# All eleven sums of down-projection weights made in the out-projection, in raw weight buffers

## The chip, the cores and the metric

The kernel runs on one core of a Trainium2 chip. The metric is the device time of one execution in microseconds (us); the time before is 2308.32 us, the median of 3 runs (2305.21 to 2309.71). All five engines of the core are in use: TensorE (PE, with its weight loads PEld), VectorE (DVE), ScalarE (ACT), GpSimd (POOL) and SyncE (SP), whose queue issues nearly all DMAs.

## The reference, cut to what matters

The kernel computes one layer of a streaming encoder for 2048 prompt tokens and 8 x 16 sample tokens, all in float32:

```python
x @ w_in -> heads (mLSTM with chunkwise state, sliding-window attention)
mix = concat(heads) @ w_out
h = layer_norm(ALPHA * x + mix)
u = h @ w_up                       # value | gate, 2 x 2816 wide
c = causal depthwise convolution of u, width 3
f = (silu(gate) * value) @ w_down  # 2816 x 1024
y = layer_norm(ALPHA * h + f)
```

Only one thing in it is touched by the change: sums of blocks of `w_down`. The big products are done by a seven-product scheme in the manner of Strassen, which needs sums and differences of quarters of the weights. For the down-projection these are made ahead of time, once, and kept in DRAM.

## The kernel before, in words

**Stages.** The program is Python that writes out every instruction. Four stages follow each other: the input projection (`i_dense`, four blocks of 512 tokens, the first with the sample tokens, 5 groups of weights), the out-projection (`o_block`, five blocks `OBLOCKS` of 3, 4, 4, 4 and 2 tiles of 128 tokens), the up-projection with the convolution (`f_ups`), and the down-projection (`f_downs`). The attention and mLSTM work of the heads runs as three chains (`t_sample`, `m_chain`, `a_chain`) that `Chains.weave` puts between the steps of the dense stages, by costs and latencies written into their `yield`s.

**Float32 in three products.** Each operand is split by `split` (L216) into a rounded part (a copy on ScalarE, L218) and a rest (a subtraction on VectorE, L219); three matmuls stand for one.

**What sets the order.** TensorE's order is that of the program text (`manual_schedule`). The instructions of the other engines, SP's DMA issues among them, are ordered by a scheduler at compile time: among what is ready, what comes earlier in the program goes first, and a DMA may go far ahead of its place if its buffer is free. On the chip each engine then works strictly through its own list. A tile of a pool has a tag, and as many buffers as the tag has; a new tile waits until an earlier one with that tag has had its last use.

**Out-projection** (L1588, `o_block`, and L901, `group`). A block is done in two halves of the 1024 output columns. A half takes the four units of 512 KB of its weights, which stay in place while the tiles of the block pass by: 8 steps of 3 matmuls (512 columns) a tile, so 24 steps in a half of block 0 and 32 in blocks 1 to 3; `steps` counts them. In the last round of a half (L919) the units are given back, and the next half's are split (`advance`, L415, `next_split`, L465, `next_raw`, L424). In a second half `x_pair` (L885) also brings in and splits the next block's tokens. A result is taken out of PSUM at L1613 and normalised by `norm` (L1562) in pieces, one every second step.

**Raw weights.** They land in `wraw`, a tag of 7 buffers of 512 KB (`WR`), by `raw_slot` (L405) and the DMA at L462, and are split from there. `raw_free` (L410) lets the program text go at most four loads ahead of the splits.

**The sums** (L841, `d_sums(k, step)`). There are 11 (`NK2`). Step 0 loads two 128 x 1024 tiles of `w_down` (L845, L846), step 1 does four subtractions of 128 x 512 on VectorE (L851 to L854), step 2 stores both tiles to `zt` (L856, L857). Before, the tiles `txy` have the tags `xr1` and `xr3`, buffers that the tokens of the input projection and `x_pair` use as well. Eight sums are made in the last two blocks of the input projection, in the four first groups of weights of each (L683); `self.sums` counts them. The other three are made in the first halves of the out-projection's blocks 1, 2 and 3, at steps 2, 14 and 20 (L1607). The down-projection reads `zt` as weights (L2015), from about 1838 us on.

Of the kernel before, what the change touches and what calls it, by code (L numbers as in the profile page):

```python
# [8 lines left out]
F32 = mybir.dt.float32  # L9
# [5 lines left out]
P = 128  # L15
D = 1024
# [21 lines left out]
WR = 7  # L38
# [16 lines left out]
NK2 = NFF // 2  # L55
# [150 lines left out]
class Prog:  # L206
# [381 lines left out]
    def i_dense(self):  # L588
        nc, a = self.nc, self.a
        nb = len(IBLOCKS)  # L590
        last = NG - 1

        self.next_raw()
        self.x_load(0, 2)
        for _ in range(3):
            self.next_raw()
        self.x_load(0, 4)
        self.single_raw = self.tp.tile([P, KD, P], F32, name="xsr", tag="pth", bufs=2)
        nc.sync.dma_start(self.single_raw, a["xs"])
        self.angles = {}  # L600
        self.rope_load(IBLOCKS[0][2], 2)
        self.rope_load(NPT, 1)
        self.next_split()
        self.x_steps(0, "b12")
        for _ in range(3):
            self.next_split()
        self.x_steps(0, 3)
        self.x_single(1, 2)
        self.x_load(0, 1)
        self.next_raw()  # L610
        self.x_load(0, 3)
        self.x_steps(0, 1)
        self.advance()
        self.x_steps(0, 2, "t3", 7, "t2", 6)
        self.x_single(4)
        self.x_steps(0, "t1", 5, "t4")
        self.sb, self.trans = {}, None

        passages = [{1: ["load"], 7: ["t3", 7], 6: ["t2", 6], 3: [3, "t4"], 4: ["b12", "t1"]},
                    {1: ["load"], 6: ["t3"], 7: [7, "t2"], 5: [6], 3: [3, "t4"], 4: ["b12", "t1"]}]  # L620
        sums = 0
        after = None
        for item in self.items:
            if after:

                after[0] -= 1
                if after[0] == 3:
                    self.logs_of(after[1] - 1)
                if after[0] < 0:
                    self.i_done = after[1]  # L630
                    after = None
            self.chains.hold = item[0] == "t" and item[1] > 0
            if item[0] == "t":
                _, b, ti, e = item
                if ("g", e, 3) not in self.wu:
                    self.advance()
                if b not in self.gates:
                    self.gates[b] = self.tp.tile([P, 5, 8], F32, name="gates", tag="gates", bufs=2)
                ps = self.bank([P, 512], "pg") if ti == 4 else self.ib[ti % 2 * 2]
                yield from self.i_direct(b, ti, e, ps)  # L640
                self.i_keys(b, ti, ps)
                if ti == 1:
                    if b + 1 < nb:
                        self.x_steps(b + 1, 1, 2)
                    else:
                        self.release(4)
                    after = [6, b + 1]
                elif ti == 3 and b or ti == 4:
                    self.release(4)
                    self.x_steps(b, 4)  # L650
                    if b:
                        self.x_steps(b, 5)
                self.advance()
                continue
            _, b, g, s = item
            if item not in self.wu:
                self.advance()
            yield from self.i_product(b, g, s)
            del self.wu[item]
            self.release(2)  # L660
            if self.trans and s != 4:
                self.i_transposes()
            with self.tc.high_priority():
                behind = self.i_after(b, g, s)
            if (b, g, s) == (0, 0, 7):
                self.t_setup()
            if (g, s) == (1, 6):
                self.rope_load(IBLOCKS[b][0], 2)
            if g == last and b + 1 < nb:
                if s == 7:  # L670
                    self.rope_load(IBLOCKS[b + 1][2], 2)
                for x in passages[b > 0].get(s, ()):
                    if x == "load":
                        self.spare = True
                        self.x_load(b + 1, 1, 2, 3, 4)
                    else:
                        self.x_steps(b + 1, x)
            if g == last and b + 1 == nb and s in (7, 5, 2, 3):
                self.x_pair(0, (7, 5, 2, 3).index(s))
            with self.tc.issue_after(behind) if behind and b == 0 else nullcontext():  # L680
                self.advance()

            if b >= nb // 2 and g < last:  # L683

                steps = (6, 2, 5) if g == last - 1 else (6, 5, 3)
                if s in steps:
                    self.d_sums(sums, steps.index(s))
                    sums += s == steps[2]
        self.sums = sums
        self.logs_of(nb - 1)  # L690
        self.chains.hold = False

# [148 lines left out]
    def d_sums(self, k, step):  # L841
        nc, V = self.nc, self.nc.vector
        if step == 0:
            self.txy = x, y = [self.xp.tile([P, D], F32, name="txy", tag=f"xr{q}", bufs=1) for q in (1, 3)]
            nc.sync.dma_start(x, self.a["wdn"][k])  # L845
            nc.sync.dma_start(y, self.a["wdn"][NK2 + k])  # L846
            return
        x, y = self.txy
        if step == 1:
            l, r = slice(0, 512), slice(512, D)  # L850
            V.tensor_sub(x[:, l], x[:, r], x[:, l])  # L851
            V.tensor_sub(x[:, r], y[:, r], x[:, r])
            V.tensor_sub(y[:, r], y[:, r], x[:, l])
            V.tensor_sub(y[:, l], y[:, l], y[:, r])  # L854
            return
        nc.sync.dma_start(self.zt[0, k], x)  # L856
        nc.sync.dma_start(self.zt[1, k], y)  # L857
# [730 lines left out]
    def o_block(self, b):  # L1588
        nc, nb = self.nc, len(OBLOCKS)
        tiles = OBLOCKS[b]  # L1590

        ys = self.ynext + [self.o_x(t) for t in tiles[len(self.ynext):]]
        self.ynext = []

        outs = [self.fp.tile([P, D], F32, name="ymix", tag="hst", bufs=2) for _ in tiles] if b == nb - 1 else ys
        for hf in range(2):
            c = slice(hf * 512, hf * 512 + 512)
            steps = 0
            for cost, ti, ps in self.group(b, tiles, 8 * b + 4 * hf, hf == 1):
                yield cost  # L1600
                if ps is None:
                    steps += 1
                    if hf and b + 1 < nb and steps == 8 * len(tiles) - 6:
                        self.ynext = [self.o_x(t) for t in OBLOCKS[b + 1][:2]]
                    if steps % 2 == 0 and self.norms and next(self.norms[0], self) is self:
                        del self.norms[0]
                    if hf == 0 and b and self.sums < NK2 and steps in (2, 14, 20):  # L1607
                        self.d_sums(self.sums, (2, 14, 20).index(steps))
                        self.sums += steps == 20
                    continue  # L1610
                y = outs[ti]
                with self.tc.high_priority():
                    nc.vector.scalar_tensor_tensor(y[:, c], ys[ti][:, c], ALPHA, ps, op0=ALU.mult, op1=ALU.add)  # L1613
                if hf and b == nb - 2 and ti >= len(tiles) - 2:

                    nc.sync.dma_start(self.zh[tiles[ti]], y)
                elif hf and b < nb - 1:
                    self.norms.append(self.norm(y, *self.ln1, self.zh[tiles[ti]]))
        assert b < nb - 1 or self.sums == NK2
        self.late = list(zip(outs, tiles))  # L1620
# [575 lines left out]
```

## Time and profile before

| | us |
|---|---|
| median of 3 runs (lowest, highest) | 2308.32 (2305.21, 2309.71) |
| profiled execution | 2306.25 |
| its span, first to last instruction | 2304.5 |
| busy: PE, DVE, ACT, POOL | 2278.9, 1807.4, 1272.4, 279.4 |
| sums in the input projection, first load to last store's issue | 299.4 to 546.2 (8 sums) |
| sums in the out-projection, likewise | 642.6 to 835.2 (3 sums) |

The profile is of one execution. Times in it are counted from the first instruction. A row of a timeline has the start, the duration, the engine, the line of the kernel, the operation, and the tiles written and read; in square brackets stands how long the engine idled before it and what released it. "w<-wraw" reads: writes `w`, reads `wraw`. A row of the list of waits has the waiting engine and line, what it waited for, the total in us, how often, and the longest. A busy TensorE is a matmul in the pipe; its idle time is what remains of a window.

### The profile page before, as it was taken

To read this page: it belongs to the slowest core of one execution; us is meant where nothing else is said; L and a number is where in the kernel's file an instruction comes from. 1 tells how busy PE (TensorE), PEld (TensorE's weight loads), DVE (VectorE), ACT (ScalarE), POOL (GpSimd) and SP (SyncE) were. 2 spreads that over 40 slices of the span, in tenths; PEclk is the share of its full clock that TensorE was granted. 3 is DMA by queue.
4 is the path that set the end of the run, shared out by engine and by line. 5 is a ranking of instruction groups with operands and counts; after the bars stand their busy time and mean duration, and the time that the engine had idled before them with its cause. 6 is when DMAs were issued, how large, how long until landed. Compare 5 with 4: busy or idle time off the path is not lost.

```text
span 2304.5 us, 39741 instructions
## 1 busy us (share of the span) xinstructions
PE 2278.9 (99%) x14293; PEld 2094.4 (91%) x14293; DVE 1807.4 (78%) x3075; ACT 1272.4 (55%) x2377; POOL 279.4 (12%) x509
## 2 busy tenths in 40 slices
PE   8999999999999999999999999999999999999998
PEld 8999999989877778999999999999999978888876
DVE  8787587787688888998778777678766786895987
ACT  5453476776766656555656555556555544444442
POOL 0001001100011210211112101003111200200200
PEclk9999999999999999999999999999999999999999
DMA  7988999899987757888777888878998786746742
GB/s 267 319 306 297 309 322 342 310 306 341 309 286 239 242 199 277 302 328 300 277 281 272 307 304 310 306 256 289 316 299 260 248 299 213 253 170 223 253 156 83
DMA packets 300165, 632.38 MB, mean 274 GB/s; under 512 B 47868, under 2 KB 141120, under 8 KB 299968
## 3 DMA queue, kind: packets, MB, share of 16 engines
q1 hardware_dynamic: 295296, 616.14, 77.3%
q0 software_dynamic: 3520, 10.56, 1.4%
q10 hardware_dynamic: 1152, 3.15, 0.4%
q8 instruction: 113, 1.85, 0.3%
q14 instruction: 84, 0.69, 0.1%
HBM read 458.11 MB, written 171.64 MB: 273 GB/s over the span
## 4 chain that ended last, share of the span: by engine, by line
PE 81%; DVE 4%; DMA 2%; issue 1%; ACT 1%; POOL 0%; SPq 0%; DVEq 0%; ACTq 0%; POOLq 0%
PE dps L1874 19%; PE fup L1874 19%; PE dps L705 8%; PE fup L2081 6%; PE dps L2081 6%; PE fht L2081 6%; PE dps L223 3%; PE dps L224 2%; PE dps L225 2%; PE ppo L1349 1%; PE psc L1304 1%; PE ppt L1343 1%; PE dps L731 1%; PE fht L1698 1%; PE pscore L1129 1%
## 5 line engine op out<-in xcount | busy, mean ns | idle before, releaser
L1874 PE MATMUL fup<-hh,uw 128*128 128x384 f32 (+1 forms) x1848 | 478.4, 328 | 0.0
L1874 PE MATMUL dps<-hh,uw 128*128 128x384 f32 (+1 forms) x1848 | 478.0, 328 | 0.0
L1874 PEld LDWEIGHTS fup<-hh,uw 128*128 128x128 f32 x1848 | 330.5, 188 | 0.0
L1874 PEld LDWEIGHTS dps<-hh,uw 128*128 128x128 f32 x1848 | 330.3, 188 | 0.0
L1932 DVE SCALAR_TENSOR_TENSOR cc<-u,cw,cc 128x768 f32<-128x768 f32 (+1 forms) x264 | 258.2, 979 | 62.8 <-ACT cc L1930 56.1
L1874 PE MATMUL fup<-hl,uw 128*128 128x384 f32 (+1 forms) x924 | 303.2, 328 | 0.9 <-DVE hl L219 0.9
L1874 PE MATMUL dps<-hl,uw 128*128 128x384 f32 (+1 forms) x924 | 302.8, 328 | 0.0
L705 PE MATMUL dps<-w,oh 128*128 128x256 f32 x1344 | 254.2, 284 | 0.0
L218 ACT CAST uw<-wraw 128x1024 fp32r<-128x1024 f32 x126 | 123.3, 979 | 230.4 <-PE dps L2081 122.4
L219 DVE TENSOR_TENSOR w<-wraw,w 128x1024 fp32r<-128x1024 f32 (+2 forms) x167 | 189.7, 1142 | 66.0 <-ACT w L218 61.9
L218 ACT CAST w<-wraw 128x1024 fp32r<-128x1024 f32 (+2 forms) x167 | 163.0, 984 | 119.0 <-PE dps L705 61.9
L705 PEld LDWEIGHTS dps<-w,oh 128*128 128x128 f32 x1344 | 210.7, 188 | 10.8 <-issue 8.1
L219 DVE TENSOR_TENSOR uw<-wraw,uw 128x1024 fp32r<-128x1024 f32 x126 | 142.5, 1131 | 62.3 <-ACT uw L218 62.2
L705 PE MATMUL dps<-w,ol 128*128 128x256 f32 x672 | 188.1, 280 | 0.0
L1874 PEld LDWEIGHTS fup<-hl,uw 128*128 128x128 f32 x924 | 173.9, 188 | 1.7 <-DVE hl L219 1.5
L2081 PE MATMUL fup<-uw,fu 128*128 128x512 f32 x726 | 174.0, 396 | 1.2 <-ACT fht L2089 1.2
L1874 PEld LDWEIGHTS dps<-hl,uw 128*128 128x128 f32 x924 | 173.8, 188 | 0.0
L705 PE MATMUL dps<-oh,w 128*128 128x256 f32 x896 | 169.6, 285 | 3.6 <-DVE w L219 1.3
L2081 PEld LDWEIGHTS fup<-uw,fu 128*128 128x128 f32 x726 | 136.6, 188 | 34.3 <-ACT fht L2089 1.6
L2081 PE MATMUL dps<-uw,fu 128*128 128x512 f32 x660 | 165.3, 396 | 1.1 <-DVE uw L219 1.1
L1930 ACT ACTIVATE cc<-u,cw 128x768 f32<-128x768 f32 (+1 forms) x132 | 132.0, 1001 | 46.2 <-DVE u L1912 22.2
L2081 PEld LDWEIGHTS dps<-uw,fu 128*128 128x128 f32 x660 | 124.1, 188 | 31.2 <-DVE uw L219 1.5
(318 smaller groups left out, 4590.0 us busy)
## 6 DMA issues: line engine op xcount, KB each, us to landing
uw<-zw SPq DMA_DIRECT2D x176, 512.0 KB, 5.1
zw<-uw SPq DMA_DIRECT2D x88, 512.0 KB, 3.3
w<-zws SPq DMA_DIRECT2D x72, 512.0 KB, 5.8
wv<-wup SPq DMA_DIRECT2D x66, 512.0 KB, 4.4
wraw<-wi SPq DMA_DIRECT2D x65, 512.0 KB, 5.5
wraw<-zt SPq DMA_DIRECT2D x60, 512.0 KB, 4.1
wraw<-wdn SPq DMA_DIRECT2D x45, 512.0 KB, 4.5
wraw<-wo SPq DMA_DIRECT2D x40, 512.0 KB, 4.7
```

The source lines that it names most:

```text
L218: nc.scalar.copy(hi, src)
L219: return nc.vector.tensor_sub(lo, src, hi.bitcast(F32)).ins
L223: mm(out, ah, bh, start=start, stop=False)
L224: mm(out, ah, bl, start=False, stop=False)
L225: mm(out, al, bh, start=False, stop=stop)
L705: mm(o, l, r, start=s in (1, 7) and c == k == i == 0, stop=k == 3 and i == 2, skip_group_check=True)
L731: mm(o, x, w, start=k == i == 0, stop=k == KD - 1 and i == 2, skip_group_check=True)
L1129: self.nc.tensor.matmul(ps[:, h], qk[:, 4 + h], qk[:, h], start=True, stop=True)
L1874: mm(ps, l[:, k], r[:, k], start=s in (1, 7) and k == 0 and i == 0, stop=k == 3 and i == 2, skip_group_check=True)
L1930: S.activation(c[:, v], u[:, 2:2 + n], AF.Identity, bias=w[3], scale=w[2])
L1932: V.scalar_tensor_tensor(c[:, v], u[:, i:i + n], w[i], c[:, v], op0=ALU.mult, op1=ALU.add)
L2081: mm(ps, l[:, k, c], r[:, k], start=s in (1, 4, 7) and u == 0 and k == 0 and i == 0, stop=u == nu - 1 and k == n - 1 and i == 2, skip_grou ...
```

## The change

The eight sums leave the input projection; its count of sums starts at 0 in the out-projection. There a first half of blocks 1, 2 and 3 makes two sums (steps 2, 10, 13 and 16, 26, 30), and every other half of blocks 0 to 3 one (steps 2, 18, 22), until there are eleven: two in block 0, three in each of blocks 1, 2 and 3. The two tiles of a sum are now taken from the seven buffers of `wraw`. The operations of a sum, their shapes and their results stay as they are.

```diff
@@ i_dense
-        sums = 0
...
-            if b >= nb // 2 and g < last:
-
-                steps = (6, 2, 5) if g == last - 1 else (6, 5, 3)
-                if s in steps:
-                    self.d_sums(sums, steps.index(s))
-                    sums += s == steps[2]
-        self.sums = sums
+        self.sums = 0
@@ d_sums
-            self.txy = x, y = [self.xp.tile([P, D], F32, name="txy", tag=f"xr{q}", bufs=1) for q in (1, 3)]
+            self.txy = x, y = [self.wp.tile([P, D], F32, name="txy", tag="wraw", bufs=WR) for _ in range(2)]
@@ o_block
-                    if hf == 0 and b and self.sums < NK2 and steps in (2, 14, 20):
-                        self.d_sums(self.sums, (2, 14, 20).index(steps))
-                        self.sums += steps == 20
+                    at = ((2, 10, 13), (16, 26, 30)) if hf == 0 and b else ((2, 18, 22),)
+                    for j in at:
+                        if self.sums < NK2 and steps in j:
+                            self.d_sums(self.sums, j.index(steps))
+                            self.sums += steps == j[2]
```

## The prediction

> **What bounds the kernel now.** First the page's parts 1 and 2: which engine fills the span.
>
> ```profile
> span 2304.5 us, 39741 instructions
> PE 2278.9 (99%) x14293; PEld 2094.4 (91%) x14293; DVE 1807.4 (78%) x3075; ACT 1272.4 (55%) x2377; POOL 279.4 (12%) x509
> ```
>
> TensorE is busy 2278.9 of 2304.5 us, and the change leaves its instructions and their order alone (the order is written out by hand, and the sums of weights hold no matmul). So the change can only take away, or add, idle time of TensorE: 25.6 us in the whole span, most of it outside the stages touched. Next the table of windows, for the second half of the input projection (where eight of the eleven sums now stand) and for each half of a block in the out-projection. The cuts lie at the eviction of a half's last tile (L1613), as this row of VectorE's timeline shows for one of them; all later rows of single instructions are from timelines too.
>
> ```profile
> 746.39 1.38 DVE L1613 SCALAR_TENSOR_TENSOR ymix<-ymix,dps 128x512 f32<-128x512 f32 x2 [0.31 <-PE dps L225]
> ```
>
> ```profile
> 296.00:625.00 329.00, 324.83 (x2728) 301.52 (x2727) 248.60 (x698) 237.10 (x603) 31.47 (x54) 1.00 0.94 324
> 628.00:653.00 25.00, 25.00 (x146) 20.92 (x143) 21.05 (x79) 14.26 (x40) 3.15 (x4) 1.00 0.95 335
> 653.00:678.50 25.50, 25.50 (x149) 19.41 (x148) 20.78 (x50) 18.27 (x44) 2.44 (x6) 1.00 0.65 218
> 678.50:713.50 35.00, 34.86 (x194) 26.81 (x194) 31.88 (x89) 23.02 (x62) 7.70 (x8) 1.00 0.87 297
> 713.50:747.50 34.00, 34.00 (x194) 26.66 (x193) 28.52 (x73) 22.87 (x58) 6.55 (x8) 1.00 0.65 208
> 747.50:781.50 34.00, 34.00 (x194) 26.40 (x193) 29.92 (x80) 20.27 (x55) 6.12 (x8) 1.00 0.69 227
> 781.50:816.00 34.50, 34.50 (x197) 27.04 (x196) 28.79 (x71) 23.04 (x59) 6.05 (x7) 1.00 0.77 264
> 816.00:850.00 34.00, 34.00 (x196) 26.84 (x195) 30.70 (x79) 20.51 (x55) 6.61 (x6) 1.00 0.54 184
> 850.00:880.00 30.00, 30.00 (x140) 22.98 (x139) 16.60 (x24) 12.64 (x24) 3.77 (x3) 1.00 0.82 284
> ```
>
> The columns: window and length, busy time of PE, PEld, DVE, ACT, POOL, granted clock, share of the DMA engines, GB/s. In the input projection TensorE idles 329.00 - 324.83 = 4.17 us, VectorE is busy 76% and the DMA engines 94%. In the out-projection it is the other way round: TensorE idles 0.14 us in all, the DMA engines have room in most halves, but VectorE is busy 81 to 91%. Work goes from a stage that lacks transfers to one that lacks VectorE. **That is the question here: 4.17 us to win, and what does a fuller VectorE cost?**
>
> **The change part by part.** *What the eight sums cost where they stand.* The list of waits of TensorE in that window:
>
> ```profile
> PE pnum L1212 <- issue: 1.9, 2, 1.4
> PE dps L705 <- ACT mr L1154: 0.8, 1, 0.8
> PE ppo L1349 <- ACT pth L1344: 0.6, 1, 0.6
> PE pht L1177 <- ACT hn L1167: 0.5, 1, 0.5
> PE pht L1177 <- DVE ql L219: 0.2, 1, 0.2
> ```
>
> None of them names a sum. But the chain of waits goes through sums, and VectorE's timeline shows how:
>
> ```profile
> 498.91 1.43 issue
> ...
> 503.82 6.30 DMA zt<-txy
> ...
> 510.14 3.58 DMA txy<-wdn
> ```
>
> ```profile
> 495.52 0.69 DVE L851 TENSOR_TENSOR txy<-txy 128x512 f32<-128x512 f32 x1 [2.91 <-DMA txy<-wdn]
> ...
> 499.55 0.69 DVE L1133 TENSOR_TENSOR dt<-pscore,dt 128x512 f32<-128x512 f32 x1
> ```
>
> ```profile
> 513.81 0.69 DVE L852 TENSOR_TENSOR txy<-txy 128x512 f32<-128x512 f32 x1 [3.55 <-DMA txy<-wdn]
> ```
>
> VectorE's queue stood 2.91 us at L851 for a load; the product `dt` (L1133) that the matmul `pnum` (L1212) reads came behind it and ended at 500.24; TensorE stood 1.43 us. At 513.81 the second load of a sum had waited for the store of the sum before (same buffer), and 3.55 us of VectorE were lost. I put 1.4 + 0.2 us down to sums by these rows, and about half of the other 2.4 us, since VectorE's order there holds sums too: a gain of 3 us, with ends 1.6 and 4.17. A loss by removal I exclude: nothing waits for a sum before the FFN's down-projection, and 32 DMA issues leave SP's queue here.
>
> *What a sum adds.* Four subtractions; two loads and two stores of 512 KB (128 x 1024 floats), each one issue of SP.
>
> ```profile
> L851 DVE TENSOR_TENSOR txy<-txy x8: 667/686/693, 311.0 to 537.0; 128x512 f32<-128x512 f32 x8
> ...
> L854 DVE TENSOR_TENSOR txy<-txy x8: 659/691/694, 316.8 to 544.9; 128x512 f32<-128x512 f32 x8
> ...
> DMA to landing us min/median/max: 3.1/5.0/8.2
> ```
>
> ```profile
> L852 DVE TENSOR_TENSOR txy<-txy x3: 635/687/694, 691.2 to 831.2; 128x512 f32<-128x512 f32 x3
> ```
>
> At 0.686 us one, a sum is 4 x 0.686 = 2.74 us of VectorE. Eight more make 21.9 us in the out-projection, 2.7 of them in the last window, which has 13.4 us free. That leaves 19.2 us for the seven windows before. The window 678.5 to 713.5 loses three operations of the old sum (2.05 us; L852 at 691.2 is the first of them) and gains two sums (5.5): 31.88 - 2.05 + 5.5 = 35.3 us of work in 35.0. The window from 816 loses one sum and gains two: 30.70 + 2.74 = 33.4 of 34. VectorE has no slack left in a first half; in the second halves it stays near 90%.
>
> *What that costs TensorE.* Nothing where an operand comes early; all of it where it comes just in time. Rows of three such places:
>
> ```profile
> 681.06 0.17 DVE L1319 RECIPROCAL asm<-asm 128x4 f32<-128x4 f32 x1
> ```
>
> ```profile
> 681.32 1.71 ACT L1321 ACTIVATE sc<-sc,asm 128x256 f32<-128x256 f32 x4 [1.20 <-DVE asm L1319]
> ```
>
> ```profile
> 682.28 0.54 PEld L1343 LDWEIGHTS ppt<-ident,sc 128*128 128x128 f32 x4 [0.26 <-ACT sc L1321]
> ```
>
> ```profile
> 739.19 0.69 DVE L1133 TENSOR_TENSOR dt<-pscore,dt 128x512 f32<-128x512 f32 x1
> ```
>
> ```profile
> 741.43 0.39 PE L1212 MATMUL pnum<-v,dt 128*128 128x129 f32 x2
> ```
>
> ```profile
> 812.68 0.15 DVE L1319 RECIPROCAL asm<-asm 128x4 f32<-128x4 f32 x1
> ```
>
> ```profile
> 814.22 1.71 ACT L1321 ACTIVATE sc<-sc,asm 128x256 f32<-128x256 f32 x4
> ```
>
> At 681 there is no slack: the reciprocal releases ScalarE, ScalarE the transposes `ppt`. At 741 it is 741.43 - 739.88 = 1.55 us, at 814 it is 814.22 - 812.83 = 1.4. The subtractions of a second half's new sum are traced at step 18 of 24 (block 0) or 32, that is at some 672, 733 and 801 us, 8 to 13 us ahead of these places and within stretches in which VectorE hardly idles. If its 2.74 us stand in front, TensorE loses 2.7 + 1.2 + 1.3 = 5.2 us; if VectorE's scheduler puts them behind, nothing. I take 4.0: all of the first place, half of the other two. The second sum of a first half (steps 16 to 30) I cost at nothing: it is covered by the 3.1 to 4.1 us in which VectorE idles in those windows; the cost without that cover is the first rival.
>
> *Buffers and queues.* The two tiles of a sum move from buffers of the tokens to the seven raw weight buffers.
>
> ```profile
> L219 DVE TENSOR_TENSOR w<-wraw,w 128x1024 fp32r<-128x1024 f32 x7 | 8.5, 1221 | 0.0
> ```
>
> ```profile
> L462 SPq DMA_DIRECT2D wraw<-wo x40: 327/333/863, 580.7 to 851.8; - x40
> ```
>
> The last load of out-projection weights is issued at 851.8, and seven splits follow after 852 (first row, VectorE's groups from 852 to 905): all seven raw buffers were full, so they are not idle; loads just run almost two halves ahead. Two or four buffers lent for some 15 us (load 5, sum 3, store 5) still leave three to five for the four units of a half, some 30 us ahead of use. I cost that at nothing; its end is a load's 5.0 us in each of seven windows, which the lead would hide. SP carries 32 more issues of 0.33 us, 10.6 us in 250, and the DMA engines 16.8 MB, which at the 184 to 297 GB/s of these windows is some 67 GB/s more over 250 us and less than the 324 of the stage it leaves.
>
> **The sum.** -3 + 4.0 = +1.0 us. The profiled execution took 2306.25 us (its span and 1.75 around it), so 2307.3; the median of the runs shown, 2308.32, lies 2.07 above it, and on that footing the forecast is **2309.3**. Its own range is 2305 (none of the 4.0) to 2313.
>
> **The rivals.** *VectorE becomes the bound (slower).* It decides from the point where a first half holds more work than time, 35.3 in 35.0 us above. VectorE's idle time there is waiting for others and stays, so the 19.2 us push TensorE. For: 81 to 91% busy before anything is added. Against: norms and sums are not urgent, and most operands come early. With half of it passed on, 9.6 - 3 = +6.6: 2314.9; all of it gives 2324.5. Chance 0.20.
>
> *The waits go and nothing comes (faster).* For: three sums and 13 norms stand in the out-projection already, at 0.14 us of idle TensorE. Against: the place at 681. All 4.17 us gone give 2304.1, 0.18% less. Chance 0.22, half of which I put beyond 0.2% because the runs themselves spread by 4.5 us.
>
> *The buffers are not there (the change does not do what it says).* The second sum of a first half gets its second tile when the first's store has landed, and VectorE stands as at 513.81: 3.55 us in three first halves on top of the forecast, +11.7: 2320. Chance 0.08.
>
> *The clock.* Stalls close together can make the granted clock fall. Three rows of the table of windows, from the start of the kernel and from the stall at 498.9:
>
> ```profile
> 38.00:41.20 3.20, 1.58 (x10) 1.19 (x10) 3.20 (x6) 3.08 (x4) 0.00 (x0) 0.95 1.02 408
> 41.20:44.60 3.40, 3.40 (x19) 3.40 (x19) 3.40 (x6) 0.81 (x1) 0.00 (x0) 0.54 0.70 218
> ```
>
> ```profile
> 498.00:501.00 3.00, 1.57 (x15) 1.40 (x14) 2.96 (x7) 3.00 (x8) 0.00 (x0) 1.00 0.76 276
> ```
>
> A stretch half idle was followed by 3.4 us at 0.54, worth 3.4 x 0.46 = 1.6 us; another half idle stretch was not. Three such falls on top of the forecast are +4.7: 2314. Chance 0.05. By the Trainium skill, "TensorE: Matmul & The Clock Gate", section "What's actually happening", the clock halves only after an idle window of about 3.4 us. By that rule stalls of at most 2.7 us would cost nothing more; the first two rows speak against it, the third agrees.
>
> **How the numbers follow.** Forecast 0.45, and the rivals 0.20, 0.22, 0.08, 0.05. A measurement of this kernel tells about 0.2% (4.6 us) from no change. Slower by more: 0.20 + 0.08 + 0.05 = 0.33, of which I move 0.01 to the middle for scatter: 0.32. Faster by more: 0.11. Within: 0.57. The range, 2303.5 to 2317, takes in the forecast, most of the faster case, and the first rival up to three fifths passed on; the buffers' rival, the rest of the first and the edge of the faster case, some 0.2, stay outside.
>
> **What would show it.** Right: TensorE's idle time from 296 to 625 us falls from 4.17 us to about 1, its list of waits from 625 to 880 shows some 4 us behind ScalarE's `sc` or VectorE's `dt`, and VectorE is busy over 95% in first halves. Wrong: no waits there (faster), waits in every half that end with VectorE (first rival), VectorE idle in front of L851 or L852 for a load (buffers), a granted clock under 1.00 after 625 us.

## The result and the profile after

The changed kernel takes **2317.77 us** (median of 7 runs, 2312.66 to 2318.9) where the kernel before takes 2308.32 beside it: ratio over all runs 1.0038 (it is not that of the two medians), 95% interval 1.0029 to 1.0047. It is slower, and 0.77 us above the range's upper end. The profiled execution took 2318.9 us.

The page of the changed kernel, its span and busy times:

```profile
span 2317.1 us, 39735 instructions
PE 2285.4 (99%) x14293; PEld 2096.1 (90%) x14293; DVE 1807.3 (78%) x3075; ACT 1273.6 (55%) x2377; POOL 277.9 (12%) x509
```

The work is the same. TensorE's 14293 matmuls stand in the same order in both traces, so each can be set against itself: its start after the change, less its start before, is a shift that grows where TensorE loses time. (All line numbers below are the changed kernel's, 7 less than before's: the sum's loads are L838 and L839, its subtractions L844 to L847, its stores L849 and L850. In the experiments some edits move the lines by one or two, and two of them start from the kernel before, with its numbers; the tile names tell what a row is.) The shift tells three stories:

| stretch (time in before's trace) | shift of TensorE, from and to | cost |
|---|---|---|
| second half of the input projection, 296 to 552 | -0.22 to -3.67 | -3.45 |
| out-projection, blocks 0 to 3, 552 to 822 | -3.67 to 1.20 | +4.87 |
| start of the last block, 870 to 900 | 1.17 to 8.61 | +7.44 |

These sum to +8.86; the ratio's 0.0038 of 2308.32 is 8.8. The rest of this execution's loss is one event at 1641, taken up at the end.

The table of windows of the changed kernel: the input projection, then the halves of blocks 1 to 3 with the start of the last block (columns as before):

```profile
296.00:625.00 329.00, 327.71 (x2755) 304.33 (x2754) 234.71 (x675) 240.23 (x606) 29.36 (x54) 1.00 0.85 277
```

```profile
676.00:714.00 38.00, 37.85 (x210) 28.97 (x209) 34.84 (x97) 23.68 (x63) 7.87 (x8) 1.00 0.92 323
714.00:748.00 34.00, 31.93 (x181) 24.54 (x180) 28.77 (x73) 22.57 (x57) 6.04 (x8) 1.00 0.89 291
748.00:783.00 35.00, 35.00 (x201) 27.25 (x200) 33.86 (x87) 20.26 (x56) 6.53 (x8) 1.00 0.81 271
783.00:818.00 35.00, 34.31 (x194) 26.30 (x193) 29.90 (x73) 22.79 (x58) 6.50 (x7) 1.00 0.94 334
818.00:851.00 33.00, 33.00 (x188) 25.88 (x187) 32.30 (x83) 20.00 (x55) 5.65 (x5) 1.00 0.76 245
851.00:882.00 31.00, 29.55 (x137) 22.39 (x135) 19.55 (x26) 9.56 (x19) 4.76 (x3) 1.00 0.92 333
```

TensorE's idle time in the input projection fell from 4.17 to 1.29 us. In the out-projection look at which halves lose: not the full ones. From 748 to 783 VectorE is busy 33.86 of 35.00 and TensorE 35.00 of 35.00; from 714 to 748 VectorE is busy 28.77 of 34 and TensorE loses 2.07. The list of waits of TensorE from 625 to 925 us names what ended them (`oh` is the rounded copy of the tokens; `zh` holds the normalised rows in DRAM, `hst` is where they are loaded again, `fht` their transposes, `hraw` a copy of these):

```profile
PE dps L223 <- ACT oh L890: 2.2, 1, 2.2
PE pnum L1205 <- DVE dt L1126: 2.1, 1, 2.1
PE fht L1693 <- ACT hraw L1694: 1.0, 1, 1.0
PE fht L1693 <- DMA hst<-zh: 0.6, 1, 0.6
```

**The loss at 741.** VectorE's timeline, then TensorE's:

```profile
723.95 0.69 DVE L845 TENSOR_TENSOR txy<-txy 128x512 f32<-128x512 f32 x1 [3.84 <-DMA txy<-wdn]
...
740.43 0.68 DVE L1126 TENSOR_TENSOR dt<-pscore,dt 128x512 f32<-128x512 f32 x1
```

```profile
741.26 0.46 PE L1205 MATMUL pnum<-v,dt 128*128 128x129 f32 x2 [2.07 <-DVE dt L1126]
```

VectorE stood 3.84 us for a sum's second load, and `dt`, behind it in VectorE's list, was late by more than its slack. Over 625 to 880 us VectorE stood 14.0 us in 8 times for loads of sums (before: 0.8 us, once). The loads are late in part because their own raw buffers are: from 625 to 846 us SP stood 6.3 us in front of L838 and L839 until a split (`w`, L219) had given a buffer back, and 2.4 us in front of L839 until an earlier sum's store had landed. The same list of waits shows the other direction:

```profile
SPq L462 <- DMA zt<-txy: 20.6, 11, 4.3
```

Eleven times SP's queue stood in front of a weight's load (L462) until a *sum's store* had landed: by this list the weight's raw buffer was one of those lent. What stands behind such a load in SP's list waits with it. Standing there is not a loss by itself: in the same stretch the kernel before stands 49.0 us in front of L462 and the changed one 36.6 us in all. Before, no store of a sum is among the releasers, and TensorE loses nothing.

**The loss at 882.** SP's timeline and its waits:

```profile
849.99 0.33 SPq L838 DMA_DIRECT2D txy<-wdn  x1
852.11 0.33 SPq L839 DMA_DIRECT2D txy<-wdn  x1
853.24 0.33 SPq L462 DMA_DIRECT2D wraw<-wo  x1
858.67 0.33 SPq L849 DMA_DIRECT2D zt<-txy  x1
860.12 0.33 SPq L850 DMA_DIRECT2D zt<-txy  x1
...
862.00 0.77 SPq L462 DMA_DIRECT2D wraw<-wo  x1
864.79 0.33 SPq L1566 DMA_DIRECT2D zh<-ymix  x1
865.22 1.21 SPq L886 DMA_DIRECT2D xraw<-zmix  x2
866.49 0.49 SPq L462 DMA_DIRECT2D wraw<-wo  x1
...
872.24 0.33 SPq L1566 DMA_DIRECT2D zh<-ymix  x1
873.17 2.43 SPq L886 DMA_DIRECT2D xraw<-zmix  x2
```

```profile
SPq L1566 <- DMA hst<-zh: 4.0, 1, 4.0
SPq L849 <- DMA txy<-wdn: 3.0, 1, 3.0
...
SPq L462 <- DMA zt<-txy: 2.4, 1, 2.4
SPq L849 <- DVE txy L845: 2.0, 1, 2.0
```

The kernel before, its four token loads:

```profile
860.09 2.40 SPq L893 DMA_DIRECT2D xraw<-zmix  x3
862.75 0.33 SPq L1573 DMA_DIRECT2D zh<-ymix  x1
863.13 0.43 SPq L893 DMA_DIRECT2D xraw<-zmix  x1
```

The eleventh sum holds two raw buffers from 850 until its stores land; the last block's weights are loaded up to 866.5 (before: 851.8), and the last two tokens of that block at 873 to 875 (before's trace has them at 862.1 and 863.1). Part of this delay is the order of SP's list: the last two token loads now stand behind a second store of `zh` (L1566, at 872.24), in front of which SP waited 4.0 us for loads of `hst` to land. In the kernel before that store comes after them (at 874.51). The list is made at compile time, so an edit of the buffers can change both the waits and the order. ScalarE, which copies the tokens, shows the end of it:

```profile
882.12 0.62 ACT L890 CAST oh<-xraw 128x512 fp32r<-128x512 f32 x1 [4.26 <-DMA xraw<-zmix]
882.95 0.62 ACT L890 CAST oh<-xraw 128x512 fp32r<-128x512 f32 x1 [0.21 <-DMA xraw<-zmix]
882.95 0.35 ACTq L1709 DMA_DIRECT2D hst<-zh  x1
```

TensorE waits for that copy. Loads of `hst`, issued from ScalarE's list behind it, end a later wait, that of the transposes `fht`. On top of the waits the clock fell (the column of the granted clock, third from the right):

```profile
880.00:883.00 3.00, 0.76 (x6) 0.53 (x5) 0.63 (x2) 0.67 (x2) 0.00 (x0) 1.00 1.02 374
883.00:886.00 3.00, 2.02 (x8) 1.23 (x8) 1.92 (x3) 2.48 (x4) 0.00 (x0) 0.64 1.02 398
886.00:889.00 3.00, 3.00 (x11) 2.41 (x11) 1.16 (x3) 2.65 (x3) 0.00 (x0) 0.50 1.02 393
889.00:892.00 3.00, 2.38 (x10) 1.68 (x9) 1.77 (x2) 0.59 (x1) 0.00 (x0) 0.73 1.03 416
```

Of the 7.4 us, 2.5 + 1.5 are lost up to the ends of the first two waits (`oh`, `hraw`). About 2.4 (four steps of the shift, 0.67 + 0.60 + 0.59 + 0.50) are matmuls at half clock, and the rest is the wait for `hst` with some more half clock.

### The profile page after: what moved, and what is told of

The parts are those of the page before. It is cut to its first block, busy times and chain, and to the rows that moved or that the text cites. A ratio compares the mean times of both kernels' runs of the same rounds, so it can differ in the third digit from the quotient of the medians.

```text
span 2317.1 us, 39735 instructions
## 1 busy us (share of the span) xinstructions
PE 2285.4 (99%) x14293; PEld 2096.1 (90%) x14293; DVE 1807.3 (78%) x3075; ACT 1273.6 (55%) x2377; POOL 277.9 (12%) x509
## 5 line engine op out<-in xcount | busy, mean ns | idle before, releaser
L219 DVE TENSOR_TENSOR w<-wraw,w 128x1024 fp32r<-128x1024 f32 (+2 forms) x167 | 189.1, 1141 | 76.8 <-ACT w L218 67.2
L219 DVE TENSOR_TENSOR uw<-wraw,uw 128x1024 fp32r<-128x1024 f32 x126 | 142.3, 1130 | 62.7 <-ACT uw L218 61.8
```

The costliest lines, as they stand in the source:

```text
L219: return nc.vector.tensor_sub(lo, src, hi.bitcast(F32)).ins
```

## The experiments

Ratios are to the kernel before on the same chip, where it took 2306.7 to 2307.7 us. Edits are to the changed kernel unless stated.

**1. Which sum costs.** Four kernels. The first lacks the last sum:

```diff
-                        if self.sums < NK2 and steps in j:
+                        if self.sums < NK2 - 1 and steps in j:
```

> Leaves out the eleventh sum, the one in the second half of block 3; the down-projection reads rows of the weights in place of it. Theory: this one sum, by its place (its loads, stores and two raw weight buffers stand ahead of the tokens and weights of the last block), costs the 7.4 us that TensorE loses around 882 to 892 us of the changed kernel. Then TensorE reaches the last block as early as at 817 us, some 1.2 us later than before, and the time falls by about 7.4 us from 2317.8 to some 2310, ratio to the kernel before 1.000 to 1.002. Rival: the whole of the sums' work fills VectorE, and one sum of eleven takes its share: 1 to 1.5 us less, ratio above 1.003, and the loss at 882 stays.

Measured: 2305.85 us, 0.9996 (0.9988 to 1.0005). One sum of eleven is worth 0.0042 of 2307.5, 9.7 us, more than the theory's 7.4 (some 2310 us was expected), and the loss at 882 is gone. The rival falls.

The second lacks the subtractions (L843 to L847 cut):

> The changed kernel without the subtractions of the sums: loads, stores and buffers are all there, VectorE does nothing for them (what is stored are the weights as loaded). Theory (the place in SP's queue, the DMA engines and the lent buffers make the last block late; in front of it VectorE's waits for the loads cost the 4.8 us of blocks 0 to 3): the loss of 2.3 us at 741 and most of the 4.8 go, the delay at 882 stays at 5 to 7 us; some 2311 us, ratio 1.001 to 1.002. Rival (VectorE's work is the cost): both go and the gain of 3.7 us of the input projection is left, 2304 to 2305 us, ratio 0.998 to 0.999.

Measured: 2311.29 us, 1.0017 (1.0008 to 1.0025). The loss at 741 is gone; that at the last block stays at 4.92 us. As the theory had it. With the subtractions gone a sum's store no longer waits for VectorE, so this edit shortens the loans as well.

The third is the kernel before with the block at its L683 cut and the count started at 8:

> The kernel before without the eight sums of the input projection (the down-projection reads rows of the weights in place of them); its three sums in the out-projection stay as before. It measures the gain alone. Theory: 3.7 us as TensorE's instructions show it at 544.7 us, and nothing given back later: 2304.6 us, ratio 0.998 to 0.999. Rival: the gain is taken back behind the input projection by another limit (loads of the out-projection's weights): ratio 0.9995 to 1.0005.

Measured: 2303.47 us, 0.9980 (0.9972 to 0.9989). The gain is real, and nothing behind takes it back.

The fourth is the kernel before with a twelfth sum, in raw weight buffers (the choice of the buffers is not shown):

```diff
+                    if hf == 1 and b == 3 and steps in (2, 18, 22):
+                        self.d_sums(NK2 - 1, (2, 18, 22).index(steps))
```

> The kernel before with one sum more: the eleventh is made a second time in the second half of block 3, at the steps and from the raw weight buffers of the changed kernel. Theory (the last sum alone makes the last block late): 5 to 8 us more, 2314 to 2316 us, ratio 1.002 to 1.0035, with the wait of the first product behind ScalarE's copy of the tokens near 880 us. Rival (the place costs only together with the fuller halves in front of it): under 1.5 us, ratio under 1.0007.

Measured: 2310.90 us, 1.0016 (1.0006 to 1.0026), with runs from 2306.12 to 2316.72. Between the two: the last sum costs something by itself (2.1 us at the last block in the trace, the last weight loaded at 862.8 in place of 866.5), but far from all that it costs in the changed kernel.

**2. Bytes, place or VectorE's work.** The last sum with 8 columns:

```diff
+            n = 8 if k == NK2 - 1 else D
-            nc.sync.dma_start(x, self.a["wdn"][k])
+            nc.sync.dma_start(x[:, :n], self.a["wdn"][k][:, :n])
```

(and so for the other load, both stores and the subtractions)

> The changed kernel with the last sum (second half of block 3) cut to 8 of 1024 columns: the same two raw weight buffers, the same two loads and two stores in SP's queue and the same four subtractions in the same order, but 1/128 of the data (the down-projection reads rows of the weights in place of it). The run without the last sum gave 2305.9 us, the changed kernel 2317.8. Theory A (what costs is the time for which the two buffers are lent and the bytes: load, subtractions and store take some 14 us, and the weights' loads and the tokens behind them in SP's queue wait that out): with tiny transfers the loan is over in a few us, and the time is that of the run without the last sum, 2305 to 2308. Rival B (the issues themselves, their order in SP's queue and the buffers being taken out of turn): most of the loss stays, 2312 us or more.

Measured: 2310.16 us, 1.0011 (1.0003 to 1.0020): neither. The expectation erred in one thing, that a tiny transfer ends the loan early. The tile's page of that sum in this kernel, and VectorE's row:

```profile
L840 SPq DMA_DIRECT2D txy<-wdn x1: 328/328/328, 849.1 to 849.1; - x1
...
DMA to landing us min/median/max: 5.3/5.3/5.3
```

```profile
854.33 0.16 DVE L845 TENSOR_TENSOR txy<-txy 128x4 f32<-128x4 f32 x1 [4.08 <-DMA txy<-wdn]
```

The same line for the last sum of the changed kernel, with whole tiles:

```profile
DMA to landing us min/median/max: 5.8/5.8/5.8
```

4 KB took 5.3 us to land, 512 KB 5.8. So the buffers were lent from 847.0 (the first load's issue) to 855.2 (the last store's) and on until it landed, against 850.0 to 860.1 in the changed kernel: 8.2 us in place of 10.1. The weights' last load went out at 857.1 in place of 866.5.

Only first halves, with three sums in each of blocks 1 to 3:

```diff
+                    at = () if hf else ((2, 8, 10), (12, 18, 20), (22, 28, 30)) if b else ((2, 8, 10), (12, 18, 20))
```

> All eleven sums in first halves: two in block 0, three in each of blocks 1 to 3; none in a second half, none in the input projection. VectorE then has 38 us of work in a first half of 35. Theory (VectorE's work is not urgent and flows into the second half, which has some 4 us free; what costs is where it stands still for a load, and the place of the last sum): up to 2 us a block, 2305 to 2309 us, ratio 0.999 to 1.0006. Rival (VectorE is the bound in first halves): the third sum passes on whole, 3 us in each of three blocks, 2311 us or more, ratio over 1.0015.

Measured: 2314.62 us, 1.0031 (1.0019 to 1.0044), as the rival had it in its sum. But 5.7 us of it fall at the start of the last block, in a half without a sum of its own. SP's timeline shows why:

```profile
852.16 0.33 SPq L849 DMA_DIRECT2D zt<-txy  x1
852.54 1.22 SPq L462 DMA_DIRECT2D wraw<-wo  x2
855.64 0.33 SPq L850 DMA_DIRECT2D zt<-txy  x1
...
865.46 1.03 SPq L462 DMA_DIRECT2D wraw<-wo  x1
```

The third sum of block 3 reaches over into that half with its two buffers, and the weights come at 865.5. And blocks 1 to 3, with three sums in each first half, cost 1.8 us together (shift 0.00 at 662, 1.79 at 822). So this run's time doesn't show VectorE as the bound. The last run below, with at most two sums in a half, speaks against it.

Ten sums, with the subtractions of second halves later:

```diff
-((2, 18, 22),)
+((2, 26, 30) if b else (2, 18, 22),)
```

> The run without the last sum (ten sums, rows of the weights read in place of the eleventh), with the subtractions in the second halves of blocks 1 and 2 at step 26 and the stores at step 30 in place of 18 and 22; the loads stay at step 2. In the run without the last sum VectorE stood 2.4 us for the load of the sum in the second half of block 1, and TensorE lost 0.95 us at 741 and 1.7 us at 808 behind dt. Theory (what costs is VectorE standing still for a load, with dt behind it): the load has landed by then, 1.5 to 2.7 us less, 2303 to 2304.5 us, ratio 0.998 to 0.9987. Rival (it is the 2.7 us of work in front of dt): the subtractions come nearer to dt, the same or slower, 2305.5 to 2308 us, ratio over 0.9992.

Measured: 2307.78 us, 1.0002 (0.9994 to 1.0011). In its trace TensorE loses nothing at 741 and 808, as the theory wanted, and blocks 0 to 3 cost 2.28 in place of 3.75, but 1.6 us at the last block come in. The median lies in the rival's range; against the run without the last sum the intervals overlap. Inconclusive in time.

Three sums left in the input projection, and eight in first halves (an edit of the kernel before; the sums from the fourth on take raw weight buffers):

```diff
+            if b >= nb // 2 and g < last and sums < 3:
...
+                    at = () if hf else ((2, 10, 13), (16, 26, 30)) if b else ((2, 8, 10), (12, 18, 20))
```

> All eleven sums are made: the first three stay in the input projection at the places and in the buffers they had before, the other eight are made in first halves only, two in each of blocks 0 to 3, in raw weight buffers; no sum in a second half. Theory: the gain of 4.0 us of the run without sums in the input projection stands at the two places at 500 and 548 us, which the later sums set (2.8 of it), and second sums of first halves cost nothing (no shift of TensorE at their places): 2304 to 2306 us, ratio 0.9985 to 0.9993. Rival (a full VectorE costs wherever the sums stand): over 2308 us, ratio over 1.000.

Measured: 2307.64 us, 1.0000 (0.9991 to 1.0008). The theory's time is missed, and the rival's bound is not reached either. Three sums that stay cost 0.7 of the 3.45 us, blocks 1 to 3 nothing, block 0 3.5.

**3. Buffers or queue.** Five sums left, six in first halves (again from the kernel before, with raw weight buffers from the sixth sum on):

```diff
+            if b >= nb // 2 and g < last and sums < 5:
...
+                    at = ((2, 10, 13), (16, 26, 30)) if hf == 0 and b else ()
```

> All eleven sums are made: the first five stay in the input projection at the places and in the buffers they had before, six are made in the first halves of blocks 1 to 3, two in each, in raw weight buffers; none in a second half and none in block 0. Theory (only the sums near 496, 510 and 537 us, at which VectorE stood 2.9 to 4.2 us for loads, cost TensorE time in the input projection; two sums in a first half of 32 steps cost nothing, since the run with three in the input projection and eight in first halves lost TensorE time in block 0 alone): most of the 4.0 us of the run without sums in the input projection, 2303.5 to 2305 us, ratio 0.998 to 0.999. Rival (the sums cost in proportion to their number wherever they stand): 2306 to 2308 us, ratio 0.9995 to 1.0005.

Measured: 2304.65 us, 0.9986 (0.9977 to 0.9994), faster than both kernels, all sums made, as the theory had it in its time. The shift of its profiled execution gives only 0.1 us; in it TensorE stood once for 2.5 us at 653. Ahead of that VectorE had stood for a load of the mLSTM chain; that one caused the other is not shown:

```profile
642.09 0.69 DVE L1111 TENSOR_TENSOR dt<-k_mcau,wi 128x512 f32<-128x512 f32 x1 [3.60 <-DMA wi<-zM]
```

From 645 to 662 us of before's trace the shift grows by 2.6 to 3.1 us in three kernels (five and six, three and eight, three in first halves) and by at most 0.5 in all others. A sum missing from block 0's second half doesn't explain it, since the kernel before has none there either. The cause stays open.

The changed kernel, with other buffers for the last sum alone:

```diff
+            pool, tags, n = (self.xp, ("xr3", "xr4"), 1) if k == NK2 - 1 else (self.wp, ("wraw", "wraw"), WR)
+            self.txy = x, y = [pool.tile([P, D], F32, name="txy", tag=q, bufs=n) for q in tags]
```

> The changed kernel with one edit: the two tiles of the last sum are the third and fourth buffer of the raw tokens in place of two raw weight buffers; its loads and stores keep their steps in SP's queue. Theory A (the lent weight buffers: raw loads of the last block's weights wait for the sum's store, SP stands in front of them, and the tokens come behind): at least half of the 9.7 us that the last sum costs goes, 2308 to 2312 us, ratio 1.000 to 1.002. Rival B (the bytes and issues of the sum in this stretch, whatever the buffer): 2314 us or more, ratio 1.0028 or more; the two last token loads now wait for the store, which would show as SP's wait in front of xraw.

Measured: 2306.04 us, 0.9993 (0.9984 to 1.0001). The bytes, the steps, the queue and the subtractions are those of the changed kernel; the whole loss of the last sum is gone, more than the theory's range had it. Its own loads no longer wait for a raw weight buffer either, so its stores go out at 850 in place of 859, and the token loads stand ahead of the second store of `zh` again. SP's timeline:

```profile
847.47 1.47 SPq L462 DMA_DIRECT2D wraw<-wo  x2
849.93 0.33 SPq L850 DMA_DIRECT2D zt<-txy  x1
851.38 0.33 SPq L851 DMA_DIRECT2D zt<-txy  x1
...
857.65 0.88 SPq L887 DMA_DIRECT2D xraw<-zmix  x2
859.28 0.33 SPq L1567 DMA_DIRECT2D zh<-ymix  x1
859.72 0.99 SPq L887 DMA_DIRECT2D xraw<-zmix  x2
```

Weights by 849, tokens by 861. **This is the run that decides: the lent weight buffers are the cause at the last block.** It doesn't separate their parts: the weights that wait for the sum's stores, the sum that waits for its own buffers, and the order that the compiler then gives SP's list.

The last sum's loads and stores issued by GpSimd (`q = nc.gpsimd if k == NK2 - 1 else nc.sync`):

> The changed kernel with one edit: the two loads and two stores of the last sum are issued by GpSimd in place of SP; the buffers are the raw weight buffers as in the changed kernel. Theory A (the loan of the buffers): the weights' loads still wait for the store's landing and SP still stands, little goes, 2314 us or more, ratio 1.0028 or more. Rival C (SP's queue stands in front of the sum's own loads and stores, 3 to 5 us in the trace, and the tokens behind them are late for that): most of the 9.7 us goes, 2308 to 2311 us, ratio 1.000 to 1.0016.

Measured: 2314.02 us, 1.0024 (1.0014 to 1.0034). Its median is 0.02 over theory A's bound and its ratio under it. The median is 3.0 us above rival C's range, whose end the interval just reaches; the trace is clearer, with 7.51 us lost at the last block as in the changed kernel. Taking the sum out of SP's queue does not free SP, which still waits for its stores (4.9 us in front of L462 from 846 to 884).

At last, no sum at all in raw weight buffers:

```diff
+            tags = ("xr1", "xr2") if k in (3, 6, 9) else ("xr3", "xr4")
+            self.txy = x, y = [self.xp.tile([P, D], F32, name="txy", tag=q, bufs=1) for q in tags]
```

> The changed kernel with one edit: no sum uses raw weight buffers. The second sums of the first halves of blocks 1 to 3 take the first and second buffer of the raw tokens, all others the third and fourth; steps and queue as in the changed kernel. The run with this edit for the last sum alone gave 2306.0 us, ratio 0.9993. Theory (what ten sums cost in blocks 0 to 3, 3.7 us between the runs without the last sum and without the sums of the input projection, is VectorE's work at tight places): the loan of weight buffers cost nothing there, so 2305 to 2307 us, ratio 0.999 to 0.9997. Rival (the loans cost there too, as at the last block): 2302.5 to 2304.5 us, ratio 0.998 to 0.9987.

Measured: 2304.73 us, 0.9994 (0.9985 to 1.0003). The ratio is in the theory's range, the median 0.27 us under it, and the rival's range begins next to it: the time cannot tell them apart. The trace speaks for the rival. Its table of windows:

```profile
676.00:714.00 38.00, 37.86 (x214) 29.45 (x213) 35.02 (x90) 23.88 (x62) 7.76 (x8) 1.00 1.00 345
714.00:748.00 34.00, 34.00 (x193) 26.61 (x193) 32.47 (x80) 23.04 (x59) 7.90 (x9) 1.00 0.93 313
748.00:783.00 35.00, 35.00 (x200) 27.26 (x199) 33.20 (x84) 22.62 (x62) 6.51 (x8) 1.00 0.90 310
```

All the sums are made here, VectorE is busy 32.47 of 34.00 us, and TensorE loses nothing in that window. VectorE stood 0.6 us for a sum's load from 625 to 880 us, in place of 14.0. Blocks 0 to 3 cost 0.95 us in place of 4.87. SP stood here too, 6.4 us in front of token loads until a sum's store had landed, and still TensorE's waits from 625 to 925 us are 1.0 us in all.

**All together.** The three stretches of the shift, as above, and the time at which the last load of out-projection weights is issued (L462). Sum of the three beside the ratio less 1, times 2307.5 us:

| kernel | 296-552 | 552-822 | 870-900 | last weight load | sum | measured |
|---|---|---|---|---|---|---|
| before | 0 | 0 | 0 | 851.8 | 0 | 0 |
| changed | -3.45 | 4.87 | 7.44 | 866.5 | 8.9 | 8.8 |
| last sum by GpSimd | -3.42 | 4.47 | 7.51 | 866.6 | 8.6 | 5.5 |
| three in first halves | -3.43 | 5.25 | 5.69 | 865.5 | 7.5 | 7.2 |
| before, plus last sum | 0.36 | -0.19 | 2.11 | 862.8 | 2.3 | 3.7 |
| no subtractions | -3.42 | 0.67 | 4.92 | 857.5 | 2.2 | 3.9 |
| last sum tiny | -3.43 | 3.93 | 4.41 | 857.1 | 4.9 | 2.5 |
| ten sums, later subtractions | -3.47 | 2.28 | 1.56 | 851.1 | 0.4 | 0.5 |
| ten sums | -3.46 | 3.75 | 0.06 | 849.5 | 0.4 | -0.9 |
| three and eight | -2.71 | 3.52 | 0.00 | 850.4 | 0.8 | 0.0 |
| five and six | -2.70 | 2.81 | 0.03 | 851.8 | 0.1 | -3.2 |
| last sum in token buffers | -3.44 | 2.48 | 0.03 | 848.6 | -0.9 | -1.6 |
| all in token buffers | -3.44 | 0.95 | 0.69 | 847.1 | -1.8 | -1.4 |
| before's three sums only | -3.42 | -0.17 | 0.69 | 847.2 | -2.9 | -4.6 |

The first column repeats to 0.05 us wherever all eight sums leave. The third is 0 to 1.6 where the last weight load goes out by 851.8 and 2.1 to 7.5 where it goes out after 857; among the latter the loss does not follow the time (4.41 at 857.1, 2.11 at 862.8). The wait that costs differs as well. Only in the changed kernel is the first wait there one for the copy of the tokens (`oh`); in the other five TensorE waits for the transposes `fht`, behind loads of `hst` (1.7 to 4.1 us) and, in two of them, the copy `hraw` too. Half-widths of the measured column's intervals are 2 to 3 us.

## Why the prediction was wrong, step by step

- **The gain**, forecast 3 us, is 3.45. Right; 1.6 of the 3 was read from rows, the rest taken as half of what remained, and that half fell out well.
- **A sum's price on VectorE**, 2.74 us, is right; so is that first halves fill up (33.86 us of 35.00, 32.30 of 33.00). What was built on it is not. "All of the first place, half of the other two" gave 4.0 and 4.87 came: 2.3 of it at the second place (741) and 0.8 just ahead of the third, some 1 in block 0, and nothing at the place without slack, 681. That the totals are near each other is luck. And the cause is another: without lent weight buffers the same work costs 0.95 us, without the work the (shorter) loans cost 0.67. By these two runs the loss needs both: loads that come late and a VectorE that stands in front of them.
- **The step that failed**: "I cost that at nothing; its end is a load's 5.0 us in each of seven windows, which the lead would hide." The lead was counted in weights, as if a late weight delayed only its own split. Its own figures give a warning: three buffers left for the four units of a half. A weight's load that waits for its buffer stops SP's queue, for sums' stores 20.6 us in 11 times, and what stands behind it has less lead: tokens of the next block, loads of the chains, the next sum's loads. At the last block the loan cost 7.4 us in place of nothing, and with other buffers for that sum 0.03. The prediction read what is queued behind a waiting instruction for VectorE (`dt` behind L851), but not for SP.
- **The last window** was costed at nothing since VectorE has "13.4 us free" there. True, and beside the point: what is scarce there is SP's queue and the lent buffers, and the eleventh sum costs 9.7 us.
- **The rivals.** VectorE as the bound (0.20) gave the right sign and, with half passed on, 2314.9, nearly the size, for the wrong reason; the run with all sums in token buffers refutes it for this amount of work. "The buffers are not there" (0.08) had the resource, and its sign came: VectorE idle in front of a sum's load, 14.0 us. Part of that is what it describes, SP waiting for a sum's tile (2.4 us for an earlier store, 6.3 for a split). What it lacks is the other direction, weights waiting for the sum, and the last block, where most of the loss lies. "The waits go and nothing comes" (0.22) had the gain; what it left out is 4.87 and 7.44 us. The clock's fall (0.05) came, as a follower of the waits.

**Left open.** At 1652 us of the changed kernel (1641 of before's trace, which has no such wait) TensorE stood 2.1 us behind ScalarE's `ua` in the up-projection and lost 4 us in all with the half clock after it. The run with before's three sums only shows the same at 1639.81 (1.95 us, 4.4 us in all), five of the other traces lose 0.7 to 1.6 us there, and the rest under 0.2. It follows no edit, and no run tested it. It is part of the 12.65 us between the two profiled executions, not shown to be part of the medians' 9.45.

## What to carry to other kernels

A buffer that looks idle belongs to the loads that will ask for it next: when it is lent, price not only the late load but the in-order queue that stands in front of it, and everything that waits behind in that queue. Read the new order of that queue too, if a compiler makes it. Here the loan was dearest where one stage ends and the next begins: look there first. And before blaming a full engine, look at whether TensorE loses time in the fullest window or in the one where the engine stands still.

## What the hardware showed that was not expected

A load of 4 KB took 5.3 us to land, one of 512 KB at the same place 5.8 (one load each): moving 1/128 of the bytes shortened the buffers' loan from 10.1 to 8.2 us only, from the first load's issue to the last store's.

The clock fell after a single stall of 2.24 us (880.55 to 882.79): the granted clock is 1.00 in a window from 883.40 to 883.80 and 0.50 in one from 884.20, ahead of the second stall, and it is 1.00 again after 890.65. After the stall of 2.07 us at 741 it stayed at 1.00 (window 714 to 748). By the Trainium skill, "TensorE: Matmul & The Clock Gate", section "What's actually happening", the array falls to half clock after an idle window of about 3.4 us, and the window is free-running. The 2.24 us are shorter than that, so here less than a whole idle window was enough.

Why one stall of two did it may lie in where they fell. The granted clock falls three times in this trace, at 40.73, 883.82 and 1651.82 us. These are 843.09 and 768.00 us apart, 247 and 225 steps of 3.4133 us; the last fall lasts one such step, the one at 883.82 two. In the five other traces with two falls these are whole numbers of the same step apart too (407, 286, 249, 247 and 247). By these traces the clock changes on a fixed grid. On it the stall at 882 lies within one step, 880.41 to 883.82, and the stall at 741 is cut in two by a step's end at 740.46: 1.27 us before it and 0.80 after. That this is the reason is an inference; no run moved a stall to test it.
